# HGRN's values turned by VectorE blocks and transfers within SBUF in place of TensorE transposes

## The chip, the cores and the metric

The kernel runs on one core of one Trainium2 chip, in one launch. The metric is the time of one execution on the device, in microseconds (us). Five engines work side by side, each through its own queue of instructions in order: TensorE (PE in the profile; PEld is its loading of weights), VectorE (DVE), ScalarE (ACT), GpSimd (POOL) and SyncE (SP). SP and POOL issue transfers (DMAs), which 16 DMA engines carry out. SBUF is the memory on the core, with 128 partitions; PSUM is where TensorE writes, in banks of 128 x 512 float32.

## The reference, cut to what matters

The kernel is one layer of a hybrid decoder: x is 2048 x 1024, float32.

```python
h = rmsnorm(x)
[hgrn columns | rwkv columns] = h @ W_in
o_hg = hgrn2(...)      # four heads of 128
o_rw = rwkv7(...)      # eight heads of 64
x = x + concat(o_hg, o_rw) @ W_out
x = x + conv_ffn(rmsnorm(x))
out = rmsnorm(x)
```

The change touches HGRN alone. For each head and each chunk of time,

```python
A = einsum('bhtk,bhsk,bhtsk->bhts', q, k, decay)
o = einsum('bhts,bhsv->bhtv', A, v) + einsum('bhtk,bhkv->bhtv', q * exp(b), S)
S = exp(b_last) * S + einsum('bhsk,bhsv->bhkv', k * exp(b_last - b), v)
```

The values v are the result of the input projection. They come out with their 128 features on the partitions and time along the free dimension; both products with v sum over time, and TensorE sums over partitions, so v is needed with time on the partitions.

## The kernel before, in words

Time is cut into four blocks of 512 steps. The first stage does the norms, the input projection, both mixers and, for three of the blocks, the output projection. The second stage does the rest, above all the feed-forward network; the change does not touch it.

The first stage is three streams of Python generators:

- `dense` does the projections. A job is one tile of 128 columns of W_in for one block: 24 matmuls of 128 x 512 (lines 270 to 272, three for each of eight pieces, since each operand is split into a high and a low part) into a "pj" bank, and then its eviction. For q, f, v and g of an HGRN head the evictions are `ev_q`, `ev_f`, `ev_v` and `ev_g`; `ev_v` (line 358) is a copy by ScalarE into the tile hv in SBUF. The weights come by POOL's queue, one job ahead. Its output blocks (`out_block`, line 379) load the mixers' results back (oraw, lines 388 and 392, on SP), split them into hh and hl and multiply by W_out.
- `rw_super` does RWKV for one block and two pairs of heads, eight times in all. It already turns two operands in the way that the change takes over: VectorE turns 32 x 32 blocks (KBb, line 754; ATb, line 765), and 16 transfers each on SP put the blocks in place (KBT, line 757; RHS, line 770). Before them it sends M's diagonal blocks through DRAM (Ed, line 745, then E, line 748), for the 31 steps of a triangular inverse on VectorE (etmp and Ti, lines 804 and 806). RHS is first read by the matmuls of line 849.
- `hg_unit` (line 946) does one head of HGRN for one block, 16 times in all. Its first step makes k = 1 - f (line 949) and VT, the turned values: four TensorE transposes of 128 x 128 into a bank of the tag "hg" (line 954), which has two banks, and one copy to SBUF by ScalarE. Then VectorE makes scaled operands for seven levels, TensorE multiplies them into A, and k is turned in the same way into KT. VT is first read by the state's matmuls (line 1057), some ten steps on, and then by the output's (line 1066). The tile SH holds the states; L1067 reads it. Near the unit's end the slot of VT is used again, for the low part of a split that line 1086 reads.

The loop at the end (line 1118) takes in turn one step of `rw_super`, one of `hg_unit` and about 2000 ns of `dense`, by costs written out by hand. That is the order in the code, and it gives each instruction its priority. The tile framework then lays the order of each engine's queue before the run: of the instructions that it reckons ready it takes the one that comes first in the code. The order is fixed on the chip, and each queue runs in order.

In this order of the code, the first step of the even units stands as follows: in units 0, 2 and 6 behind the transfers into KBT and ahead of those into RHS of the same round; in units 8, 10 and 12 behind both; in units 4 and 14 ahead of both and of Ed. `dma` is SP's queue and `store` POOL's.

Lines such as L122, L247, L248, L254 and L255 are helpers (`act`, `split_to`, `split`), used from many places: the names of the tiles tell which place it is.

Of the kernel before, what the change touches and what calls it, by code (L numbers as in the profile page):

```python
# [7 lines left out]
F32 = mybir.dt.float32  # L8
# [3 lines left out]
AF = mybir.ActivationFunctionType  # L12
# [6 lines left out]
P = 128  # L19
# [48 lines left out]
def tile_layer(ctx, tc, consts, x, norm1_w, w_in, hg_lb_logits, hg_norm_w, rw_shift_mu, rw_w0, rw_w2,  # L68
# [4 lines left out]
    V, S, TE = nc.vector, nc.scalar, nc.tensor  # L73
    dma, store = nc.sync.dma_start, nc.gpsimd.dma_start
# [11 lines left out]
    ident = cp.tile([P, P], F32, name="ident")  # L86
# [27 lines left out]
    def act(out_, in_, func, **kw):  # L114

        want = tables.get(func)
        if want is not None and want != tab["now"]:
            pre = S.preload_act_table_set(want)
            for u_ in tab["uses"]:
                tc.add_manual_dep(pre.ins, u_.ins.name, NOSYNC, reason="table order")  # L120
            tab.update(now=want, pre=pre, uses=[])
        i_ = S.activation(out_, in_, func, **kw)  # L122
        if want is not None:
            tc.add_manual_dep(i_.ins, tab["pre"].ins.name, NOSYNC, reason="table order")
            tab["uses"].append(i_)
        return i_
# [119 lines left out]
    def split_to(hi, lo, src):  # L246
        c_ = S.copy(hi, src)  # L247
        return c_, V.tensor_sub(lo, src, hi.bitcast(F32))  # L248
# [25 lines left out]
    def phase1(c1):  # L274
# [3 lines left out]
        rp = c1.enter_context(tc.tile_pool(name="rp", bufs=1, reuse_waits="tile"))  # L278
# [18 lines left out]
        def bank(kind):  # L297
            return ps.tile([P, 512], F32, tag=kind, name=kind, bufs=2)
# [647 lines left out]
        def hg_unit(nb, j):  # L946
            q, f, v, gg = (stage.pop((n_, nb, j)) for n_ in "qfvg")
            k = rp.tile([P, BLK], F32, tag="hk", name="hk")
            V.tensor_scalar(k, f, -1.0, 1.0, ALU.mult, ALU.add)

            VT = rp.tile([P, 4, P], F32, tag="VT", name="VT")
            tp = bank("hg")
            for b in range(4):
                TE.transpose(tp[:, b * P:(b + 1) * P], v[:, b * P:(b + 1) * P], ident)
            act(VT, tp.rearrange("p (b t) -> p b t", t=P), AF.Copy)
            yield
            A = rp.tile([P, 4, 32], F32, tag="hA", name="A")
            Pf = f
# [84 lines left out]
            tp = bank("hg")  # L1043
# [9 lines left out]
            SH = rp.tile([P, 5, P], F32, tag="SH", name="SH")  # L1053
            V.tensor_copy(SH[:, 0, :], Sc[:, j, :])
            sps = bank("hg")
            for b in range(4):
                TE.matmul(sps[:, b * P:(b + 1) * P], KT[:, b, :], VT[:, b, :], start=True, stop=True)
            for b in range(4):
# [5 lines left out]
            for b in range(4):  # L1064
                ts_ = slice(b * P, (b + 1) * P)
                TE.matmul(op[:, ts_], VT[:, b, :], Af[:, b, :], start=True, stop=False)
                TE.matmul(op[:, ts_], SH[:, b, :], q[:, ts_], start=False, stop=True)  # L1067
            sq = rp.tile([P, BLK], F32, tag="hk", name="osq")
            act(sq, op, AF.Square)
            hi, lo = (rp.tile([P, BLK], F32R, tag=tag, name="part") for tag in ("Sf", "VT"))  # L1070
            split_to(hi, lo, sq)
# [22 lines left out]
        def hg_stream():  # L1094
            for n in range(4 * NBLK):
                while ready["hg"] <= n:
                    yield None
                yield from hg_unit(n // 4, n % 4)
# [47 lines left out]
    with ExitStack() as c2:  # L1146
# [36 lines left out]
        with tc.tile_pool(name="op", bufs=1, reuse_waits="tile") as op_:  # L1183
# [7 lines left out]
            b = NBLK - 1  # L1191
# [311 lines left out]
    with tc.tile_pool(name="dn", bufs=1, reuse_waits="tile") as dn:  # L1503
# [61 lines left out]
        for s_ in range(DS, N):  # L1565
            g, p, kk = steps[s_]
# [60 lines left out]
```

## Time and profile before

| | before |
|---|---|
| median of three runs | 2648.05 us (2644.51 to 2653.97) |
| the profiled execution, its own time | 2645.14 us |
| its span, from first to last instruction | 2643.1 us |
| clock granted to TensorE, mean | 0.992 |
| DMA queue of SP (q1), share of the 16 engines' span | 41.3% |
| DMA queue of POOL (q0) | 21.1% |

A line of a group has the source line, the engine, the operation, out<-in by tile names, the shapes and the count; behind the bar stand the busy time in us and the mean of one in ns, then the engine's idle time just before and what ended it. A line of a timeline has the start and the duration in us, and in brackets the idle time before. The lines of SP (SPq) are the issuing of transfers: they tell how long SP was held, not when the data landed. A matmul's duration includes the time in which the next one already runs behind it, so the distance between starts tells what one costs.

### The profile page before, as it was taken

The page shows a single profiled execution, that of the slowest core. Times are in us where ns is not written, and L with a number is a line of the kernel's source. Part 1 is how long each engine was busy: PE and PEld are TensorE (multiplying, and loading weights), DVE is VectorE, ACT ScalarE, POOL GpSimd, SP SyncE. Part 2 cuts the span into 40 slices and gives each one's busy share as a digit, 9 for nine tenths or more (in the row PEclk, how much of TensorE's full clock was granted, in tenths as well). Part 3 has the DMA queues.
Part 4 walks back from the last instruction along what each step waited for, and adds up shares of the span by engine and source line. Part 5 has one row for each costly group of instructions (what it writes and reads, how often), then busy time and mean ns, then how long its engine had stood idle before and what let it go on. Part 6 is the DMA issues. An engine that isn't in the chain of part 4 may idle for free. (4 is left out here: it accounts for less than half of the span.)

```text
span 2643.1 us, 51079 instructions
## 1 busy us (share of the span) xinstructions
PE 2545.1 (96%) x19403; PEld 2044.3 (77%) x19403; DVE 1973.0 (75%) x3760; ACT 1356.5 (51%) x2242; POOL 381.1 (14%) x686
## 2 busy tenths in 40 slices
PE   7999999999999899999899999999999999999998
PEld 5877777767777667777678888787888887888887
DVE  4978576676676765787678799987998887766556
ACT  5565444555445554354466754556554544545444
POOL 6433222212222122232100000000000000000000
PEclk9999999999999999999999999999999999999999
DMA  8847464656665566856574477747764553998665
GB/s 305 243 161 204 141 173 128 149 152 212 191 180 145 168 212 184 262 167 164 188 260 136 129 233 255 230 152 228 245 204 130 169 172 128 337 318 280 204 192 187
DMA packets 415115, 523.18 MB, mean 198 GB/s; under 512 B 149280, under 2 KB 245910, under 8 KB 414870
## 3 DMA queue, kind: packets, MB, share of 16 engines
q1 hardware_dynamic: 360337, 341.59, 41.3%
q0 software_dynamic: 54464, 178.32, 21.1%
q8 instruction: 152, 2.49, 0.4%
q14 instruction: 94, 0.76, 0.1%
q10 hardware_dynamic: 68, 0.02, 0.0%
HBM read 372.99 MB, written 134.22 MB: 192 GB/s over the span
## 5 line engine op out<-in xcount | busy, mean ns | idle before, releaser
L270 PE MATMUL pj<-hh,wh 128*128 128x512 f32 x960 | 392.3, 409 | 4.7 <-ACT rkv L122 2.1
L271 PE MATMUL pj<-hl,wh 128*128 128x512 f32 x960 | 379.1, 395 | 0.0
L272 PE MATMUL pj<-hh,wl 128*128 128x512 f32 x960 | 378.3, 394 | 0.0
L270 PE MATMUL ua<-Bh,uwh 128*128 128x512 f32 x704 | 276.9, 393 | 6.7 <-ACT m L122 5.8
L272 PE MATMUL ua<-Bh,uwl 128*128 128x512 f32 x704 | 274.5, 390 | 0.0
L271 PE MATMUL ua<-Bl,uwh 128*128 128x512 f32 x704 | 274.3, 390 | 0.0
L270 PEld LDWEIGHTS pj<-hh,wh 128*128 128x128 f32 x960 | 181.2, 189 | 53.7 <-issue 9.0
L272 PEld LDWEIGHTS pj<-hh,wl 128*128 128x128 f32 x960 | 181.3, 189 | 39.3 <-issue 0.3
L271 PEld LDWEIGHTS pj<-hl,wh 128*128 128x128 f32 x960 | 181.5, 189 | 35.1 <-issue 0.6
L254 ACT CAST uwh<-uraw 128x512 fp32r<-128x512 f32 x220 | 134.1, 617 | 128.7 <-PE ua L271 54.1
L255 DVE TENSOR_TENSOR dal<-draw,dah 128x512 fp32r<-128x512 f32 x138 | 95.4, 691 | 107.0 <-ACT dah L254 106.7
L255 DVE TENSOR_TENSOR uwl<-uraw,uwh 128x512 fp32r<-128x512 f32 x220 | 147.6, 687 | 33.7 <-ACT uwh L254 33.6
L254 ACT CAST dah<-draw 128x512 fp32r<-128x512 f32 x138 | 85.6, 621 | 159.2 <-PE da L271 74.0
L270 PEld LDWEIGHTS ua<-Bh,uwh 128*128 128x128 f32 x704 | 132.2, 188 | 38.3 <-ACT m L122 10.6
L272 PEld LDWEIGHTS ua<-Bh,uwl 128*128 128x128 f32 x704 | 132.2, 188 | 28.0 <-DVE uwl L255 0.4
L271 PEld LDWEIGHTS ua<-Bl,uwh 128*128 128x128 f32 x704 | 132.3, 188 | 26.7
L270 PE MATMUL ud<-Bh,uwh 128*128 128x512 f32 x352 | 138.1, 392 | 0.0
L1497 POOL DMA_DIRECT2D gd<-y x2 | 1.1, 540 | 947.9 <-DVE y L1495 947.9
L272 PE MATMUL ud<-Bh,uwl 128*128 128x512 f32 x352 | 137.2, 390 | 0.0
L271 PE MATMUL ud<-Bl,uwh 128*128 128x512 f32 x352 | 137.1, 390 | 0.0
L271 PE MATMUL da<-dbl,dah 128*128 128x512 f32 x332 | 129.5, 390 | 0.2 <-DVE dbl L255 0.2
L272 PE MATMUL da<-dbh,dal 128*128 128x512 f32 x332 | 129.3, 389 | 0.0
(581 smaller groups left out, 6191.6 us busy)
## 6 DMA issues: line engine op xcount, KB each, us to landing
uraw<-in_w_up_dram SPq DMA_DIRECT2D x176, 256.0 KB
woraw<-in_w_out_dram POOLq DMA_DIRECT2D x96, 256.0 KB, 3.4
br<-gd SPq DMA_DIRECT2D x88, 256.0 KB
draw<-Sg SPq DMA_DIRECT2D x88, 256.0 KB
draw<-Tw SPq DMA_DIRECT2D x88, 256.0 KB
gd<-y SPq DMA_DIRECT2D x86, 256.0 KB
Sg<-br SPq DMA_DIRECT2D x72, 256.0 KB
xt<-x1d SPq DMA_DIRECT2D x32, 512.0 KB
```

The source lines that it names most:

```text
L254: S.copy(hi, src)
L255: V.tensor_sub(lo, src, hi.bitcast(F32))
L270: TE.matmul(acc, lh, rh, start=first, stop=False, skip_group_check=skip)
L271: TE.matmul(acc, lh, rl, start=False, stop=False, skip_group_check=skip)
L272: TE.matmul(acc, ll, rh, start=False, stop=last, skip_group_check=skip)
L1497: (dma if end is None else nc.gpsimd.dma_start)(gd_[2 * h + b][fb * P:(fb + 1) * P, :], ys[0][:, b * BLK:(b + 1) * BLK])
```

## The change: values turned on VectorE and by SP's transfers

The copy of v from its bank by ScalarE (`ev_v`) stays. In the unit's first step, the four TensorE transposes, their "hg" bank and ScalarE's copy go. VectorE turns hv in 32 x 32 blocks into a new tile vb, which shares the slot of SH, and 16 transfers on SP, each of 32 partitions by 4 pieces of 32 elements, put the blocks into VT.

```diff
@@ hg_unit, first step
+            vb = rp.tile([P, 4, 4, 32], F32, tag="SH", name="vb")
+            V.transpose(vb.rearrange("p a b c -> p b a c"), v.rearrange("p (b a t) -> p b a t", a=4, t=32))
             VT = rp.tile([P, 4, P], F32, tag="VT", name="VT")
-            tp = bank("hg")
-            for b in range(4):
-                TE.transpose(tp[:, b * P:(b + 1) * P], v[:, b * P:(b + 1) * P], ident)
-            act(VT, tp.rearrange("p (b t) -> p b t", t=P), AF.Copy)
+            for g in range(4):
+                for a in range(4):
+                    dma(VT[32 * a:32 * a + 32, :, 32 * g:32 * g + 32], vb[32 * g:32 * g + 32, a])
             yield
```

## The prediction, made before the change was run

> **What bounds the kernel now.** I read the page first: its first lines, then the same engines over the mixer stage alone (65 to 1300 us, where all sixteen HGRN units run), since only that stage is changed.
>
> ```profile
> span 2643.1 us, 51079 instructions
> PE 2545.1 (96%) x19403; PEld 2044.3 (77%) x19403; DVE 1973.0 (75%) x3760; ACT 1356.5 (51%) x2242; POOL 381.1 (14%) x686
> core 0: us, PE busy (x) PEld busy (x) DVE busy (x) ACT busy (x) POOL busy (x), PEclk, DMA share, GB/s
> 65.00:1300.00 1235.00, 1173.53 (x13364) 920.62 (x13363) 878.27 (x2084) 607.14 (x1027) 323.78 (x584) 0.98 0.61 179
> ```
>
> In the stage TensorE is busy 1173.5 of 1235 us, so it idles 61.5 us. VectorE is busy 71%, ScalarE 49%, the DMA engines 61%. TensorE is the bound, and what remains is spread over many short waits, of which the largest are these (TensorE's waits in the stage; total, times, longest):
>
> ```profile
> PE pj L270 <- ACT hh L247: 7.1, 6, 1.9
> PE rw L823 <- DVE TZ L810: 5.5, 2, 4.0
> PE rw L907 <- DVE M L886: 4.9, 2, 2.8
> ```
>
> No wait on KBT or RHS, the two tiles that already get their data by 16 transfers each, is among TensorE's waits: those transfers are hidden today.
>
> **What is removed.** First the four TensorE transposes of a unit (timeline of TensorE in unit 0, the first of 16).
>
> ```profile
> 95.05 0.39 PE L271 MATMUL pj<-hl,wh 128*128 128x512 f32 x1
> 95.28 0.39 PE L272 MATMUL pj<-hh,wl 128*128 128x512 f32 x1
> 95.51 0.60 PE L954 MATMUL hg<-ident,hv 128*128 128x128 f32 x4
> 95.86 0.48 PE L270 MATMUL pj<-hh,wh 128*128 128x512 f32 x1
> 96.18 0.39 PE L271 MATMUL pj<-hl,wh 128*128 128x512 f32 x1
> L954 PE MATMUL hg<-ident,hv 128*128 128x128 f32 x64 | 10.6, 288 | 0.8 <-ACT osq L122 0.8
> L122 ACT ACTIVATE VT<-hg 128x512 f32<-128x512 f32 x16 | 9.5, 595 | 5.7 <-PE hg L954 5.6
> ```
>
> Durations overlap, so I count starts. Dense matmuls follow each other every 0.23 us (95.05, 95.28). From the L272 at 95.28 to the second dense matmul after it (96.18) is 0.90 us; without the transposes it would be 0.46. One unit therefore costs TensorE 0.44 us, sixteen cost **7.0 us**. The upper bound is the group's whole busy time and the idle before it, 10.6 + 0.8 = 11.4 us. The lower is nothing, where TensorE would only wait in their place. I take 7.0, because most of the stage is dense matmuls on both sides as here.
>
> The copy VT<-hg leaves ScalarE: 16 x 0.595 = 9.5 us. ScalarE is only 49% busy, so this lies beside other work; I count 0 (bound: the 7.1 us in which TensorE waits for ScalarE's hh). A bank of the two "hg" banks is no longer taken at the unit's start, which can only end the 0.8 us wait counted above.
>
> **What is added on VectorE.** One 128x512 transpose in 32x32 blocks a unit. The kernel has the same shape already, on AT:
>
> ```profile
> L765 DVE STREAM_TRANSPOSE ATb<-AR 128x512 f32<-128x512 f32 x16 | 10.9, 694 | 0.0
> ```
>
> 16 x 0.694 = 11.1 us, an increase of 1.3% on 878. If every one held up TensorE it would cost 11.1 us; if none did, 0. TensorE's two larger waits on VectorE (5.5 + 4.9) are 10.4 us of 878 busy, so VectorE rarely decides: I take **+1**. The new buffer vb shares the slot of SH, whose last readers are the matmuls L1067 of the unit before; they are over before v is turned (unit 1's come ahead of its own first step), so I count that wait at nothing. If it were not over, the etmp steps on VectorE's queue would stand behind it. VT's own slot was used by the low part that L1086 reads at the end of the unit before: SP now waits for that where ScalarE did, with oT's stores and RHS behind it; by code order that reader is over as well, and I count 0.
>
> **What is added on SP.** 16 transfers a unit, 256 in all, each 32 partitions by 4 pieces of 128 B. The nearest row is RHS<-ATb, 32 partitions by 8 such pieces (issue time on SP, min/median/max), and the SP queue shows how issues follow each other in the first pair:
>
> ```profile
> L770 SPq DMA_DIRECT2D RHS<-ATb x128: 585/610/2811, 116.2 to 1214.6; - x128
> 96.06 2.03 SPq L745 DMA_DIRECT2D Ed<-M  x4
> 98.13 1.78 SPq L757 DMA_DIRECT2D KBT<-KBb  x2
> 101.04 1.44 SPq L748 DMA_DIRECT2D E<-Ed  x2
> 102.52 13.57 SPq L757 DMA_DIRECT2D KBT<-KBb  x10
> 116.19 15.36 SPq L770 DMA_DIRECT2D RHS<-ATb  x16
> ```
>
> At 0.61 us a unit holds SP for 9.8 us; at the rate of the last row (15.36 / 16 = 0.96) 15.4 us. I take 0.61, since each transfer has half the pieces: 256 x 0.61 = 156 us of SP in 1235. SP has the room on average, but in bursts: from 102.5 to 131.5 it issues without a pause. Landing takes about 3 us more (Ed's last issue ends at 98.09, E, which needs it, starts at 101.04).
>
> SP issues in order, so what stands behind VT's 16 is late by up to 9.8 us: KBT, RHS, the loads oraw and xh, the stores x1d and oT. RHS in pair 0 would end at 131.55 + 9.8 + 3 = 144.4; its first reader runs at 143.70, so this one place may lose 0.7 us. The place that matters most is the start of the two output blocks, where oraw already stands directly behind RHS and TensorE's largest wait (7.1 us, on hh, made from oraw) lies:
>
> ```profile
> 143.70 0.43 PE L849 MATMUL rw<-RHS,TTs 64*64 64x128 f32 x2
> 526.84 11.51 SPq L770 DMA_DIRECT2D RHS<-ATb  x16
> 538.45 15.45 SPq L388 DMA_DIRECT2D oraw<-oT  x4
> 552.28 0.79 PE L270 MATMUL pj<-wh,hh 128*128 128x512 f32 x1
> 860.33 11.09 SPq L770 DMA_DIRECT2D RHS<-ATb  x16
> 871.52 19.04 SPq L388 DMA_DIRECT2D oraw<-oT  x4
> 888.28 0.50 PE L270 MATMUL pj<-wh,hh 128*128 128x512 f32 x1
> ```
>
> First use comes 13.8 us (552.28) and 16.8 us (888.28) after the issue. Taking off 9.8 leaves 4.0 and 7.0, about one landing and two casts: tight, not broken. I take 0.5 us in each block and the 0.7 of RHS, **+2** rounded up; bounds 0 and 2 x 9.8 = 19.6.
>
> DMA engines: 256 x 128 = 32,768 packets more of under 512 B.
>
> ```profile
> DMA packets 415115, 523.18 MB, mean 198 GB/s; under 512 B 149280, under 2 KB 245910, under 8 KB 414870
> ```
>
> That is 22% more of the small ones, with the engines 61% busy in the stage. The weight loads on POOL's queue cover this, as they run a job ahead; I count 0. If that cover went, the dense matmuls would wait on wh and wl.
>
> **The sum.** -7.0 + 1 + 2 = -4 us. The profiled run took 2645.14 us, its span of 2643.1 and 2.0 around it, so 2641.1 by its own time. The median of the three runs, 2648.05, lies 2.9 above it; the forecast in its terms is **2644**.
>
> **Two rules of the Trainium skill.** VectorE transposes and the TensorE ones compare, for one unit, as 0.694 us and 9.8 us of SP against 0.44 us and 0.595 us of ScalarE. The Trainium skill, page "VectorE: DVE Perf Modes", section "Rules for kernel authors", says to use TensorE for a 128x128 transpose where a PSUM destination will do; by it the change is wrong, and rival A is the form that this would take here. Length speaks for the rule, the idle room of VectorE and SP against it.
>
> TensorE's weight loads fill 920.6 of 1235 us, 75%, against 95% for matmuls. The Trainium skill, "Perfetto Trace Analysis", section "Identifying the Most-Contended Engine", calls matmul busy time a bad measure and weight-load time a good one; by it TensorE would have a quarter of its time free and the 7.0 us might be worth nothing (rival C). The even 0.23 us between dense starts speaks against that.
>
> **Rivals.** *A, VT comes late and holds TensorE (slower).* VT is read by L1057. Counting through the loop that hands out the steps, VT's transfers stand behind KBT's in unit 0 and behind RHS's as well in units 8, 10 and 12.
>
> ```profile
> 124.79 0.38 PE L1057 MATMUL hg<-VT,KT 128*128 128x128 f32 x2
> 728.13 15.12 SPq L770 DMA_DIRECT2D RHS<-ATb  x16
> 742.13 1.05 PE L1057 MATMUL hg<-VT,KT 128*128 128x128 f32 x8
> 882.20 1.16 PE L1057 MATMUL hg<-VT,KT 128*128 128x128 f32 x8 [0.63 <-ACT KT L122]
> 1061.79 13.12 SPq L770 DMA_DIRECT2D RHS<-ATb  x16
> 1078.14 1.05 PE L1057 MATMUL hg<-VT,KT 128*128 128x128 f32 x8
> ```
>
> With 9.8 us of issue and 3 of landing, VT is there at 116.2 + 12.8 = 129.0, 743.3 + 12.8 = 756.1, 871.4 + 12.8 = 884.2 and 1074.9 + 12.8 = 1087.7: late by 4, 14, 2 and 10 us, 30 in all. If L1057 keeps its place, TensorE stands for these 30 us, and the time is 2644 + 30 = **2674**; half of it gives 2659. It decides as soon as VT lands after KT's copy. Against it: KBT's issues (98.13) are seen ahead of E's (101.04), though they come later in the code, so the order is laid by what the planner reckons ready, and dense matmuls can be put ahead of L1057; a late unit then only eats the pause before the next one.
>
> *B, the output blocks pay.* oraw late by the full 9.8 us, twice, beyond the 1 us counted: 2644 + 18.6 = **2663**. For: oraw is directly behind RHS. Against: the 4 and 7 us of margin.
>
> *C, no gain.* TensorE's freed slots turn into waits on the chains of VectorE: 2648 + 1 + 2 = **2651**. For: 61.5 us of idle are already such waits. Against: dense matmuls stand on both sides of the slot.
>
> **How the numbers follow.** About 0.3% of this kernel, 7.9 us, is what a measurement can tell from no change: faster is below 2640.1, slower above 2656.0. Forecast 0.55 (its own range 2635, the 11.4 us and one more of noise, to 2650, both counted costs doubled), A 0.2, B 0.1, C 0.15. Faster: 0.27, all from the forecast. Same: 0.28 of it, all but 0.02 of C, 0.03 of A and 0.02 of B, 0.46. Slower: the rest, 0.27. The range runs from 2635 to 2664: it takes in B whole and A up to two thirds.
>
> **What would show it.** Right: no L954 and no VT<-hg; TensorE's busy time in the stage some 7 to 10 us less; VectorE's 11 more with a transpose of about 0.69 us; 256 more issues on SP of about 0.6 us; TensorE's waits within a few us of 61.5; L1057 not waiting for VT. Wrong: a row in which L1057 waits for a transfer into VT (A); the wait on hh grown by over 5 us (B); TensorE's busy time down while the stage's end stays (C); issues nearer 1 us, which moves all of A's times.

## The result, and the profile after

| | before | after |
|---|---|---|
| median, four runs each, on one chip | 2648.11 us (2644.51 to 2653.97) | 2665.84 us (2661.45 to 2666.57) |
| ratio, with 95% interval | 1 | 1.0061 (1.0040 to 1.0083) |
| the profiled execution, its own time | 2645.14 us | 2666.57 us |

The changed kernel is slower by 0.6%, some 16 us by the ratio and 18 by the medians. It does what it says: the transposes of line 954 and their copy are gone, and so are their durations from the sum; the new rows stand at the sizes that were forecast (page of the changed kernel, and the tile view of VT; in the changed kernel lines after 952 stand one or two later than before, so the state's matmuls are L1058, HGRN's store L1081).

```profile
span 2664.8 us, 51360 instructions
PE 2552.6 (96%) x19339; PEld 2047.6 (77%) x19339; DVE 1988.0 (75%) x3776; ACT 1347.3 (51%) x2226; POOL 381.1 (14%) x686
DMA packets 451982, 527.41 MB, mean 198 GB/s; under 512 B 186144, under 2 KB 282774, under 8 KB 451734
L952 DVE STREAM_TRANSPOSE vb<-hv 128x512 f32<-128x512 f32 x16 | 11.3, 705 | 0.3
```

```profile
L956 SPq DMA_DIRECT2D VT<-vb x256: 585/600/1967, 119.2 to 1253.6; - x128
its engine sat idle before it (us, times) until:
  issue: 3.8, 10
  DMA RHS<-ATb: 1.3, 1
  ACT KT L122: 1.2, 2
```

The second fence says that TensorE's readers of VT stood for a transfer once, for 1.3 us, at 133.28 us in unit 0. The row names the transfers into RHS, but the matmul does not read RHS, and VT's last issue had ended at 131.22: it is VT that it waited for. This is all that TensorE itself stood for VT. Yet it lost time in two ways. Its idle time, span less busy, grew from 98.0 (2643.1 - 2545.1) to 112.2 us: +14.2. Its busy time grew by 7.5 although the transposes left it. Against the kernel without the transfers (experiment 1), which runs the same 19339 matmuls in 2537.5 us, it is 15.1 us longer for the same work. The granted clock says why (the view by cores; 0.992 before).

```profile
core 0: 2664.8 us, clock 0.985
```

0.015 x 2664.8 = 40.0 us of clock were not granted, against 0.008 x 2643.1 = 21.1 before: 19 more, as an estimate (the clock is rounded to 0.001, so each end may be off by 1.3). A part of that fell into the gaps themselves, where there was nothing to slow.

**Where it stood.** TensorE's waits in the stage (65 to 1320 us; total, times, longest):

```profile
PE rw L823 <- DVE TZ L810: 18.3, 6, 8.4
PE hg L993 <- DVE hk L949: 10.4, 4, 5.4
PE pj L270 <- ACT hh L247: 6.0, 5, 2.9
```

TZ grew from 5.5 to 18.3 us, hk is new among TensorE's larger waits, hh did not grow. Two places are typical. The first is at the second output block; these are SP's issues, then VectorE's last step of the inverse, then TensorE, all of the changed kernel:

```profile
867.63 11.62 SPq L770 DMA_DIRECT2D RHS<-ATb  x16
879.29 11.81 SPq L956 DMA_DIRECT2D VT<-vb  x16
891.21 1.01 SPq L388 DMA_DIRECT2D oraw<-oT  x2
```

```profile
894.56 1.04 DVE L810 STREAM_TRANSPOSE TZ<-Ti 128x512 f32<-128x512 f32 x1 [0.23 <-DMA oraw<-oT]
```

```profile
886.61 0.68 PE L1049 MATMUL hg<-hX 128*64 128x64 f32 x8
895.65 1.08 PE L823 MATMUL rw<-TZ,M 32*32 32x32 f32 x64 [8.36 <-DVE TZ L810]
```

The same two steps in the kernel before:

```profile
891.97 1.05 DVE L810 STREAM_TRANSPOSE TZ<-Ti 128x512 f32<-128x512 f32 x1
893.07 0.25 PE L823 MATMUL rw<-TZ,M 32*32 32x32 f32 x4 [1.51 <-DVE TZ L810]
```

Before, the loads into oraw were issued from 871.52 on; now they stand behind VT's 16, 19.7 us later. Before, the inverse's last step came at 891.97, so it is late by 2.6 us only; but in the meantime TensorE did the output block, from 888.28 on. Now oraw is not there, the last matmul of the projection starts at 885.85, and TensorE stands for 8.36 us until the inverse is done; the output block starts at 904.99. The wait carries the name of TZ; the missing cover is the output block. The stretches of the changed kernel, and below them those of the kernel before, show what follows:

```profile
core 0: us, PE busy (x) PEld busy (x) DVE busy (x) ACT busy (x) POOL busy (x), PEclk, DMA share, GB/s
886.00:896.00 10.00, 1.64 (x40) 1.26 (x41) 9.01 (x30) 3.29 (x6) 1.07 (x2) 0.74 0.44 118
896.00:904.00 8.00, 6.49 (x152) 5.51 (x142) 3.44 (x9) 4.02 (x10) 0.00 (x0) 0.50 0.01 2
904.00:912.00 8.00, 8.00 (x45) 6.50 (x44) 6.16 (x13) 4.05 (x7) 0.54 (x1) 0.98 0.45 128
```

```profile
886.00:896.00 10.00, 6.99 (x92) 4.68 (x91) 9.36 (x28) 7.01 (x14) 0.54 (x1) 1.00 0.41 137
896.00:904.00 8.00, 6.56 (x84) 4.48 (x85) 6.68 (x15) 5.84 (x13) 0.54 (x1) 1.00 0.55 166
```

After the gap the clock (the column behind POOL's) is 0.50 for 8 us, where before it was 1.00. TensorE is busy for 6.49 of these 8 us, so the gap of 8.4 us costs about 3 us more behind it (an estimate: half of 6.49).

The second place is in unit 9. VT's 16 issues are in two parts, with HGRN's store of the unit before between them:

```profile
768.94 4.46 SPq L956 DMA_DIRECT2D VT<-vb  x7
773.50 0.54 SPq L1081 DMA_DIRECT2D oT<-osq  x1
```

```profile
779.88 0.43 DVE L949 TENSOR_SCALAR hk<-hf 128x512 f32<-128x512 f32 x1 [3.80 <-DMA oT<-osq]
```

```profile
780.36 0.65 PE L993 MATMUL hg<-hq,hk 128*32 128x32 f32 x32 [5.40 <-DVE hk L949]
```

VectorE had osq ready at 772.56 (its last product). The store left 0.94 us later, behind seven of VT's issues. hk has osq's slot, so it waits until the store has landed, and starts 6.4 us after the store's issue; before, it started 2.5 us after it:

```profile
758.25 0.33 SPq L1080 DMA_DIRECT2D oT<-osq  x1
760.77 0.42 DVE L949 TENSOR_SCALAR hk<-hf 128x512 f32<-128x512 f32 x1
```

So most of this wait is the store's landing, and not its place in the queue; what slowed the landing is not shown. TensorE stands 5.40 us for hk. osq itself was 14 us later than before (772.56 against 758.23), as all of unit 8 was late by then.

VT's own slot plays a part here too. SP stood with unit 9's first transfer at the head of its queue from 751.88 to 768.92, until unit 8's last reader of the low part in VT's slot was done (L1087; waits of SP in the stage, SP's L956 being VT's transfers):

```profile
SPq L956 <- PE hg L1087: 19.7, 3, 17.0
```

**When it was lost.** The ends of the sixteen evictions hv (ScalarE's copies out of the bank) mark the progress of the projection: units 0 to 9 lie between 3.8 us earlier and 4.2 us later than before, units 6 to 9 1.5 to 3.0 us earlier. Units 10 and 11 are 6.2 and 5.7 later, 12 to 15 between 15.1 and 16.9, and the second stage's first matmul (ua) is 22.5 us later. So the change was ahead in the first half of the stage, and lost all of it and more in the second. In units 8, 10 and 12 VectorE stood too, for the state's matmuls (VectorE's waits in the stage):

```profile
DVE SH L1060 <- PE hg L1058: 15.7, 4, 5.7
```

### The profile page after: what moved, and what is told of

Same layout as the page of the kernel before. It is cut to its first block, busy times and chain, and to the rows that moved or that the text cites. A ratio compares the mean times of both kernels' runs of the same rounds, so it can differ in the third digit from the quotient of the medians.

```text
span 2664.8 us, 51360 instructions
## 1 busy us (share of the span) xinstructions
PE 2552.6 (96%) x19339; PEld 2047.6 (77%) x19339; DVE 1988.0 (75%) x3776; ACT 1347.3 (51%) x2226; POOL 381.1 (14%) x686
## 2 busy tenths in 40 slices
DMA packets 451982, 527.41 MB, mean 198 GB/s; under 512 B 186144, under 2 KB 282774, under 8 KB 451734
## 4 chain that ended last, share of the span: by engine, by line
PE 53%; issue 18%; DVE 10%; DMA 7%; ACT 5%; POOL 4%; SPq 1%; POOLq 0%; DVEq 0%; ACTq 0%
PE pj L270 5%; PE pj L271 4%; PE pj L272 4%; PE ua L270 4%; PE ua L272 4%; PE ua L271 4%; PE da L270 3%; PE da L271 3%; PE da L272 3%; POOL wl L575 2%; PE db L271 2%; PE db L272 2%; PE db L270 2%; PE ud L272 2%; PE ud L270 2%
```

## The experiments

Times are medians. Each kernel is compared with the kernel before as run beside it, whose median was 2643.9 to 2648.1 in the five groups; ratios are given with 95% intervals.

**1. The transfers left out** (e1, its edit here against the changed kernel; values only half turned).

```diff
-            vb = rp.tile([P, 4, 4, 32], F32, tag="SH", name="vb")
-            V.transpose(vb..., v...)
             VT = rp.tile([P, 4, P], F32, tag="VT", name="VT")
-            for g in range(4):
-                for a in range(4):
-                    dma(VT[32 * a:32 * a + 32, :, 32 * g:32 * g + 32], vb[32 * g:32 * g + 32, a])
+            V.transpose(VT..., v...)
```

> VectorE turns the 32x32 blocks straight into VT and the 16 transfers are left out (the blocks stay in the wrong places, so the values are only half turned). Queue theory (the 16 issues on SP make oraw, RHS and stores late, TensorE is left without work and its clock is halved): only the gain is left, 2648 less about 7, 2636 to 2645 us, and no gap of TensorE over 4.5 us before L823. Rival, VectorE (the added transposes hold up the chain that L823 waits for): 2650 to 2660 us. Rival, VT late (the HGRN chain is late by itself): as the queue theory here, 2636 to 2645.

Measured 2632.14 us, ratio 0.9956 (0.9940 to 0.9973): 11.8 us faster, and below the expected 2636. Its page:

```profile
span 2633.0 us, 50956 instructions
PE 2537.5 (96%) x19339; PEld 2036.7 (77%) x19339; DVE 1981.4 (75%) x3776; ACT 1349.0 (51%) x2226; POOL 380.7 (14%) x686
```

TensorE stands 1.9 us for TZ in the stage, and for hk hardly at all. All that is removed, and VectorE's transpose, are in this kernel; so the transpose costs little if anything, the gain is larger than forecast, and the transfers turn -12 into +16 or so. With them vb is left out, which held the slot of SH, and SP's wait for VT's slot. VectorE stands for the transfers out of vb for 9.6 us in the changed kernel (three times, before it may write SH). Experiment 2, which has neither, shows that they are not needed for the loss.

**2. The kernel before, with the transfers added** (e2): 16 a unit from hv into a spare tile, at the same place in the code; nobody reads them.

```diff
             act(VT, tp.rearrange("p (b t) -> p b t", t=P), AF.Copy)
+            v4 = v.rearrange("p (b a t) -> p a b t", a=4, t=32)
+            for g in range(4):
+                for a in range(4):
+                    dma(spare[32 * a:32 * a + 32, :, 24 * g:24 * g + 24], v4[32 * g:32 * g + 32, a, :, 0:24])
             yield
```

> The kernel before, TensorE transposes kept, with 16 transfers a unit from hv into a spare tile that nobody reads, of the same count of pieces (128, of 96 B), issued on SP at the same place in the code. Queue theory: the loss without the gain, 2648 plus 18 to 25, 2660 to 2675 us. Rival, VT late: nobody waits for these transfers, 2645 to 2652. Rival, VectorE: no VectorE work is added, 2645 to 2652.

Measured 2667.85 us, ratio 1.0092 (1.0073 to 1.0111): +24 us, with nothing that waits for the data. So VT's own lateness (rival A) is not needed for a loss of this size. The loss comes in the same stretches as in the changed kernel: the evictions hv of units 8 and 9 are 1.7 and 1.9 us later than before, of units 10 and 11 9.1, of units 12 to 15 20.8 to 21.6. TensorE's waits bear other names, though: the largest is for M (7.3 us), TZ has 5.9, and hk is not among the larger ones. The slot of hv is held longer too, but ScalarE stands for it only once, 4.8 us before 537.31, where no time is lost. SP's issues at the second output block:

```profile
880.13 11.06 SPq L960 DMA_DIRECT2D spare<-hv  x16
891.29 2.33 SPq L389 DMA_DIRECT2D oraw<-oT  x2
```

**3. One transfer in place of 16** (e5): as 2, with the same 2048 pieces of 96 bytes in one transfer a unit.

```diff
+            v4 = v.rearrange("p (n t) -> p n t", t=32)
+            dma(spare.rearrange("p b (g t) -> p (b g) t", t=24), v4[:, :, 0:24])
```

> The kernel before with one transfer a unit from hv into the spare tile, on SP, with the same 2048 pieces of 96 B that the 16 transfers of e2 moved. Queue theory (the time for which 16 issues hold SP is what costs): one issue costs almost nothing, 2642 to 2650 us. Rival, DMA engines (the 2048 small pieces a unit slow the other transfers): the loss of e2 stays, 2660 to 2670.

Measured 2646.79 us, ratio 0.9994 (0.9981 to 1.0008): nothing. The tile views of e2 and e5:

```profile
L960 SPq DMA_DIRECT2D spare<-hv x256: 585/599/1857, 84.7 to 1252.0; - x128
```

```profile
L958 SPq DMA_DIRECT2D spare<-hv x16: 600/669/1387, 85.8 to 1221.0; - x16
```

One issue of all pieces takes 0.67 us, 16 issues of a sixteenth each 0.60 us apiece. The DMA engines got the same pieces both times; what costs is the issues.

**4. The transfers at the unit's end in the code** (e10): as 2, but behind the store of oT.

> The kernel e2 (before, with 16 transfers a unit into a spare tile), its transfers handed out at the unit's end and not at its start. The same 256 issues on SP. If the place matters (ahead of RHS and of oraw), most of e2's loss goes: 2644 to 2656 us. If the sum of the time on SP matters: as e2, 2662 to 2675.

Measured 2649.74 us, ratio 1.0011 (0.9997 to 1.0025). The same 256 issues, still about 0.6 us each, now cost 3 us and not 24. So it isn't SP's total either: it is where they stand in its queue. The second output block shows it, kernel by kernel (from the timelines of SP and of TensorE):

| | oraw's first issue | the block's first matmul |
|---|---|---|
| before | 871.52 us | 888.28 us |
| without transfers (e1) | 871.11 us | 885.74 us |
| changed | 891.21 us | 904.99 us |
| before, with 16 transfers (e2) | 891.29 us | 907.61 us |
| with one transfer (e5) | 872.17 us | 892.13 us |
| at the unit's end (e10) | 878.06 us | 894.93 us |

**5. Another queue**: the 16 transfers of the changed kernel on ScalarE's queue (e6, `S.dma_start`) and on POOL's (e13, `nc.gpsimd.dma_start`).

> The kernel after, its 16 transfers a unit issued from ScalarE's queue instead of SP's. Queue theory: RHS, oraw and the stores of oT are on time again, the gaps of TensorE near 548 and 887 us go, and ScalarE is held for some 10 us a unit, for which it has room in most places: 2635 to 2652 us. Rival, DMA engines: 2660 to 2670. Rival, VT late in its chain: VT now lands earlier, so faster than after as well, but the gaps at the output blocks stay.

> The kernel after with its 16 transfers a unit on POOL's queue, which carries the weights and none of RHS, oraw and oT. If only what stands behind the transfers on SP costs: 2636 to 2650 us. If any queue has something that suffers (here the weight loads, as ScalarE's evictions did in e6): 2660 to 2690.

ScalarE's: 2685.78 us, ratio 1.0145 (1.0129 to 1.0160), worse than SP's; the expectation failed. ScalarE's own evictions now stand behind the issues (tile view of VT: the issues, and the largest of those that wait for VT):

```profile
L956 ACTq DMA_DIRECT2D VT<-vb x256: 592/612/1632, 93.8 to 1281.3; - x128
  ACT sgm L122: 58.4, 6
```

POOL's: 2654.81 us, ratio 1.0032 (1.0014 to 1.0050), 0.55 us an issue; between the two expectations: about half of the loss is gone, and 7 us stay. POOL's queue carries the projection's weights. VectorE stands 25.8 us there for the transfers out of vb, whose slot SH needs, against 9.6 us in the changed kernel; what carries the 7 us was not tested.

**6. Half of the units** (e3: even ones, e4: odd ones; the others as before).

> The change in the even units alone (whose transfers meet KBT, RHS and oraw on SP), the odd ones as before. Queue theory: most of the loss, 2653 to 2664 us. Rival, VT late: VT is late in even units only, so the same or more, 2655 to 2668. Rival, VectorE: half of the loss, 2655 to 2659.

> The change in the odd units alone, the even ones as before. Queue theory: the smaller part, since only stores of oT stand behind these transfers and later oraw loads in the output blocks: 2644 to 2656 us. Rival, VT late: odd units read VT over 15 us after it has landed, so no loss and half of the gain, 2642 to 2648. Rival, VectorE: half of the loss, 2655 to 2659.

Even: 2658.48 us, ratio 1.0054 (1.0037 to 1.0071). Odd: 2655.97, 1.0040 (1.0025 to 1.0054). These times lie in the ranges of several theories at once, so they decide little. The halves cost +14.5 and +12 us, together more than the whole; so neither the pairing with RHS (even units) nor any price per unit explains it, and parts do not add up.

**7. Fewer issues by way of DRAM** (e7): four writes of vb and four reads.

```diff
+            Vd = dp.tile([32, 16, P], F32, tag="Vd", name="Vd", bufs=2)
             for g in range(4):
-                for a in range(4):
-                    dma(VT[32 * a:32 * a + 32, :, 32 * g:32 * g + 32], vb[32 * g:32 * g + 32, a])
+                dma(Vd[:, :, 32 * g:32 * g + 32], vb[32 * g:32 * g + 32].rearrange("p a b c -> p (a b) c"))
+            for a in range(4):
+                dma(VT[32 * a:32 * a + 32], Vd[:, 4 * a:4 * a + 4])
```

> The kernel after with the blocks sent through DRAM: four writes and four reads, 8 issues on SP in place of 16 (the same 2048 pieces of 128 B, then 128 rows of 2 KB). Queue theory: SP is held for about half of the time or less, so under half of the loss beside the gain: 2638 to 2652 us. Rival, DMA engines: more bytes than after, 2660 to 2675.

Measured 2664.80 us, ratio 1.0064 (1.0049 to 1.0079): the expectation failed, half of the issues cost as much. One reason that the trace shows: each unit's reads stand on SP until its writes have landed, 28.0 us in all, and what is behind them stands too (waits of SP in the stage; L958 is the reads):

```profile
SPq L958 <- DMA Vd<-vb: 28.0, 15, 4.5
```

VT also comes later this way. At the second output block (SP's issues and TensorE's steps of e7):

```profile
880.20 6.58 SPq L388 DMA_DIRECT2D oraw<-oT  x2
```

```profile
892.62 1.08 PE L823 MATMUL rw<-TZ,M 32*32 32x32 f32 x64 [8.19 <-DVE TZ L810]
899.54 0.79 PE L270 MATMUL pj<-wh,hh 128*128 128x512 f32 x1
```

oraw was issued 11 us earlier than in the changed kernel, yet TensorE still took the inverse's matmuls first, for which it stood 8.19 us, and the output block's only at 899.54. That raised a second theory: the order laid before the run is worse, whether or not the data is there.

**8. The order pinned** (e11: e7 with a dependence that puts L823 of the second pair behind the output block's first two pieces; e12: the changed kernel with the same).

```diff
+                if s_ == 1 and nb - 1 in pinned:
+                    tc.add_manual_dep(z_.ins, pinned[nb - 1].ins.name, NOSYNC, reason="output block first")
```

> The kernel e7 (through DRAM) with one constraint for the planner: in the second and fourth pair of the two middle blocks, the matmuls L823 come behind the first two pieces of the output block on TensorE's queue. In e7 oraw had been issued at 880 us, yet TensorE stood from 884 to 893 for L823 with the output block queued behind it. If the laid order is the cause there, that gap goes: 2648 to 2659 us. If oraw really is late, TensorE waits for it in the same place: 2660 to 2668.

> The kernel after with the same constraint. Here oraw is issued only at 891 us, behind RHS and VT, about when TZ is made. If real lateness on SP is the cause, the gap stays and only its name changes, 2660 to 2670 us. If the laid order is the cause here too, 2650 to 2659.

e11: 2660.39 us, 1.0049 (1.0031 to 1.0067). e12: 2665.09 us, 1.0065 (1.0047 to 1.0083), no different from the changed kernel. In e11 TensorE's waits are now led by the output block's own data:

```profile
PE pj L272 <- DVE hl L248: 12.2, 2, 9.3
```

So the gap moves from one name to the other. In these runs the order alone was not at fault at this place: both the inverse and the output block were late. In e12 TensorE did stand for VT, once, for the 5.2 us before 891.09.

**9. The transfers spread** two at a time over the unit's first steps (e9).

> The kernel after with its 16 transfers handed out two at a time over the first steps of the unit, not all in the first one. The number of issues and their time on SP are the same. If it is the burst that costs (16 issues in one piece ahead of RHS, oraw or a store), part of the loss goes: 2650 to 2660 us. If it is the sum of the time on SP, nothing changes: 2662 to 2668.

Measured 2689.49 us, ratio 1.0159 (1.0138 to 1.0180), the worst of all, outside both expectations. The state's matmuls come 7 to 67 us later than before, and TensorE's waits in the stage are led by

```profile
PE rw L823 <- DVE TZ L810: 26.2, 7, 9.1
```

The number of issues is the same as in the changed kernel, and each unit's last now comes some steps later. So here VT's lateness is a likely part of the cost; no run separates it.

**10. What stands behind VT's issues, moved out of their way, one by one**: the loads into oraw on ScalarE's queue (e8); TZ in a dead part of another tile, so that it needn't wait for RHS's transfers, whose source has TZ's slot (e14); HGRN's stores on POOL's queue (e15); all three (e16).

```diff
-                            dma(raw, oT[nb][k * P:(k + 1) * P, :])
+                            S.dma_start(raw, oT[nb][k * P:(k + 1) * P, :])
...
-            TZ = tile_("XH", [16, 16, 2], "TZ")
+            TZ = AT[:, 0].rearrange("p c (m f) -> p c m f", f=2).rearrange("p c (n m) f -> p (c n) m f", m=16)
...
-            last_dma(nb)(oT[nb][j * P:(j + 1) * P, :], sq)
+            nc.gpsimd.dma_start(oT[nb][j * P:(j + 1) * P, :], sq)
```

> The kernel after with the loads oraw of the output blocks on ScalarE's queue, so that they do not stand behind RHS and VT's transfers. Queue theory, with the output blocks as its dearest place: the gaps of 5.2 us near 548 and 8.4 us near 887 shrink to under 3, and 2650 to 2660 us remain (the wait for the store of oT near 775 stays). Rival, the inverse's chain is late by itself (TZ behind RHS): the gaps before L823 stay, 2662 to 2668.

> The kernel after with TZ in the part of AR that is no longer read, and not in the slot of RHS's source, so that TZ need not wait for the 16 transfers into RHS. In after TZ came up to 11 us after its last etmp step (pairs 0, 2, 4 and 6). If this wait carries the loss: 2648 to 2658 us. If the output blocks and the stores carry it (their pairs, 3 and 5, show no such wait): 2660 to 2668.

> The kernel after with HGRN's stores of oT on POOL's queue in all blocks, so that the slot that k needs is not held by a store that stands among VT's transfers. If this carries a part: the gap of 5.4 us near 775 goes, 2653 to 2661 us. If not: 2662 to 2668.

> e8, e14 and e15 together: oraw on ScalarE's queue, TZ in a free place, the stores on POOL's queue. If these three carry the loss, only the gain is left: 2632 to 2648 us. If half of it lies elsewhere (VT late in the HGRN chain, the slots of other tiles): 2650 to 2660.

| | time | ratio |
|---|---|---|
| e8, oraw | 2660.39 us | 1.0052 (1.0037 to 1.0067) |
| e14, TZ | 2678.57 us | 1.0110 (1.0087 to 1.0133) |
| e15, stores | 2667.54 us | 1.0071 (1.0048 to 1.0094) |
| e16, all three | 2654.85 us | 1.0026 (1.0011 to 1.0041) |

Alone, oraw's move seems to give a little (its interval overlaps that of the change): the 8.36 us for TZ at the second output block are gone, and 4.82 us for hh stand there instead (hh is made from oraw). TZ's makes it worse, and the stores' gives nothing: the gap of 5.4 us is gone from its place, but the waits on hk total 12.5 us all the same. All three together bring the loss down to 7 us. TZ's slot, as a cause by itself, falls. The waits of e14:

```profile
PE rw L823 <- DVE AR L810: 18.2, 7, 8.4
```

TensorE's waits of e8:

```profile
PE pj L270 <- ACT hh L247: 13.5, 7, 6.0
PE rw L823 <- DVE TZ L810: 5.9, 5, 3.6
```

**11. The first two blocks, the last two** (e17: the change for units 0 to 7, e18: for 8 to 15).

```diff
+            if nb < 2:                      # e18: nb >= 2
                 vb = rp.tile([P, 4, 4, 32], F32, tag="SH", name="vb")
...
+            else:
+                VT = rp.tile([P, 4, P], F32, tag="VT", name="VT")
+                tp = bank("hg")
...
```

> The change in units 0 to 7 (the first two blocks) alone, TensorE's transposes kept in units 8 to 15. If the loss belongs to the last two blocks, where SP also carries oraw, xh, x1d and the norm's loads: half of the gain and no loss, 2640 to 2648 us, which would be no slower than before. If every block pays alike: 2652 to 2660.

> The change in units 8 to 15 alone. If the loss belongs to the last two blocks: 2662 to 2674 us, all of it. If every block pays alike: 2652 to 2660.

e17: 2639.21 us, ratio 0.9979 (0.9967 to 0.9991). e18: 2659.35 us, 1.0047 (1.0033 to 1.0062). In the first half the change gains 5.5 us (0.2%); in the second it costs 14.7 us by the medians and 12.4 by the ratio, with the first half left as it was. Both together make +7 to +9, and the whole change +16 to +18, so here too the parts do not add up. The page of e17, and TensorE's waits in e18:

```profile
span 2636.8 us, 51222 instructions
PE 2541.3 (96%) x19371; PEld 2039.6 (77%) x19371; DVE 1977.5 (75%) x3768; ACT 1354.0 (51%) x2234; POOL 381.5 (14%) x686
```

```profile
PE rw L823 <- DVE TZ L810: 15.2, 5, 8.0
PE hg L1000 <- DVE hk L949: 9.2, 4, 4.4
```

e18 has the two waits of the changed kernel, at nearly their size. e17's idle time, 2636.8 - 2541.3 = 95.5 us, is 2.5 below that of the kernel before, and its clock is 0.992 as before. e17 is faster than both kernels. SP's long wait for VT's slot belongs to the second half: 15.2 us in e18, at most 2.0 in e17. VectorE's wait for the transfers out of vb stands in e17 too (7.0 us), and it is fast all the same.

## Why the prediction was wrong

Forecast were 2644 us and a range of 2635 to 2664; measured were 2665.8. Likeliest was "same", and it is slower.

- *TensorE's transposes, -7.0.* On the small side. The kernel without transfers gained 11.8 us by medians, 7 to 16 by the interval; the bound was 11.4. In its profiled execution busy time is 7.6 us below the kernel before (2537.5 against 2545.1), which is the 7.0; the other 2.5 us of its span are idle time that went, and it had been put at 0.8.
- *VectorE, +1.* Right for the transpose: 0.705 us each against 0.694, and the kernel without transfers shows no loss. The slot of SH was counted at nothing; VectorE stood 9.6 us for the transfers out of vb there, which e17 shows to be no great matter (7.0 us, and faster).
- *DMA engines, 0.* Right as far as tested: experiment 3 is level with the kernel before. The packets of under 512 B grew by 36,864 (186144 - 149280), not by 32,768.
- *SP, +2, "tight, not broken".* **This step failed.** The duration was right (0.600 us against 0.61), and so was the queue behind it: oraw stands behind RHS and then VT. But between experiment 1 and the changed kernel the ratios differ by 0.0105, which is 28 us, not 2. Four things were missing. First, the price was taken at one place, oraw, with the margins of the kernel before. Those margins hold only if RHS ends where it did: it ended at 871.5 before and at 879.3 after, as the steps before it were already late, and oraw came 19.7 us later and not 9.8. Secondly, a store of HGRN stands among VT's issues, and its landing gives hk its slot; the stores were named, but not priced. Thirdly, SP's wait for VT's slot was put at nothing, since by the order of the code its last reader was over: it was not, and SP stood for it 19.7 us, 17.0 of them at unit 9. What that alone costs was not tested; experiment 2, whose transfers take the slot of no other tile, loses as much. Fourthly, a stall was priced at its own length. Idle time grew by 14.2 us, but the slower work took about as much again.
- *The wait on hh as the sign of it.* Wrong: that row fell from 7.1 to 6.0 us. The delay shows under the names of TZ and hk, since TensorE's order puts those ahead.
- *Rival A, VT late.* VT came late where it was forecast (in units 8 and 10 its issues ended at 749.34 and 891.10 us, where before its first readers ran at 742.13 and 882.20), but TensorE stood for it only 1.3 us, in unit 0. As the argument against it said, the order was laid anew: the first matmul of the state in unit 8 came at 762.17, against 742.13 before. That a late unit "only eats the pause" held for units 0 to 7, where these matmuls are between 4 us earlier and 9 us later; in units 8, 10 and 12 they are 20 to 38 us later. There it is VectorE that stands for them, 4.6 to 5.7 us each time, before it updates the states (0.8 us in all before). So A's mechanism may carry a part of the loss; experiment 2 shows that a loss of the size comes without it.
- *Rival B, the output blocks pay.* Nearest, with 2663: same queue and same place, but by another wait. Its number is near in part by luck, since the gain (12, not 7) and the cost (28, not 22) were both larger. It had 0.1.
- *Rival C.* The transposes' slots were worth something: falls.

What is shown: the transfers cost, not the turning (experiment 1); their issues, not their bytes (2 against 3); their place in SP's queue, not their sum (4); and most of it in the last two blocks (11). What stays open: how the 28 us divide. By the ratios, oraw's move alone gave -2 us, TZ's +13 and the stores' +3, all three together -9, so no single one carries it; each move also lays another order, and what that alone is worth is not known. VT's own lateness is not excluded as a part of it, as experiments 7 and 9 were not explained by the number of issues. Why the first two blocks bear the same issues was not settled either. A gap of 5.16 us for TZ stands there as well, at the first output block (553.78 us; 5.15 in e17, which is faster all the same), and the progress of the projection still shows them 1.5 to 3.0 us ahead. One difference is SP's long wait for VT's slot, which only the second half has.

## What to carry to other kernels

Price an added transfer by what stands behind it in its queue, and follow each to the end: the load that becomes a later job's operand, and the store whose landing gives a slot back; then ask what TensorE has to do if that comes late. Ask the same of the slots that a new transfer waits for, since it stands at the head of its queue meanwhile. Where a queue is busy in bursts, count issues and not bytes, and try the new path in a part of the kernel alone: here the change for the first half of the units is 0.2% faster than the kernel before. A gap of TensorE is to be priced with the slower clock behind it.

## What the runs showed of the hardware

- Behind a gap of 8.4 us TensorE's granted clock was 0.50 for 8 us and back at 0.98 in the next 8. The Trainium skill, page "TensorE: Matmul & The Clock Gate", section "Why this matters for your kernels", asks for no gaps over some 3 us between bursts, since the clock then falls back to half; the trace agrees.
- An issue of small pieces on SP took about the same whatever their number: 0.600 us for 128 pieces (the changed kernel), 0.599 (e2), 0.669 for 2048 (e5); one of 32 rows of 2 KB took 0.420 (e7). POOL's took 0.549 and ScalarE's 0.612 for 128 pieces. The Trainium skill, page "DMA: Bandwidth & Descriptors", section "Issuing engines are not separate DMA queues", says that issuing from several engines saves only the sequencer's time, usually small beside the transfer. Here that time was what counted: 16 issues where one would do took 24 us of the kernel's time (e2 against e5).
